# When GpSimd drains at the end of a windowed attention kernel: behind its last instruction, or behind the landing of its own stores

## The chip, the cores and the metric

One core of one Trainium2 chip. The metric is the device time of one execution in microseconds (us), as the median of several runs. Of each kernel one execution was also taken with the hardware profiler; its span (first to last instruction) is about 2 us shorter than its time. Where a kernel was looked at once, its state is called unknown: its time is quoted without a verdict, and the argument rests on its trace alone.

## The reference

Attention within windows of 64 rows, for four sequences of 4096 rows and 1536 columns:

```python
q_w = q.reshape(B, nw, W, D)          # W = 64; k_w and v_w alike
logits = np.einsum('bnwd,bnud->bnwu', q_w, k_w) * D ** -0.5
attn = softmax(logits)                # over the last axis
out = np.einsum('bnwu,bnud->bnwd', attn, v_w).reshape(B, S, D)
```

## The kernel before

The 16,384 rows are worked off in N = 32 blocks of 512. GpSimd issues nearly all transfers: it loads q, k and v of block u + 2 (cast to 16 bits on the way), copies what has landed into the working tiles, and stores the results of block u - 1. Each transfer adds 16 to a semaphore when it has landed. Only the last block is stored by SP (SyncE), in two halves. At the end SP clears all semaphores, and before that GpSimd has to be drained, as a later drain of GpSimd still looks at the semaphores of its transfers. So the drain can be moved, but not just dropped.

```python
for u in range(1, N):
    hand_over("q", u, q16, m_q, g_q)       # wait for the landing, copy, request block u + 2
    hand_over("k", u, k16, m_k, g_k)
    ...                                    # cut: order of the last but two block
    gp.wait_ge(m_q, u + 1)
    store(u - 1)                           # signals d_o[(u - 1) % 3]
    hand_over("v", u, v16, m_v, g_v)
...
for i, c in enumerate((1, 3)):             # the last block, in two halves, by SP
    for a in range(2):
        sy.wait_ge(n_e[a], c)
    sy.dma_start(...).then_inc(d_l[i], 16)
gp.drain()
gp.sem_inc(done, 1)
sy.wait_ge(done, 1)
for i in range(NO):                        # NO = 3
    last = max(u for u in range(N - 1) if u % NO == i)
    sy.wait_ge(d_o[i], 16 * (last // NO + 1))
for i in range(2):
    sy.wait_ge(d_l[i], 16)
sy.sem_clear(range(lo, hi + 1))
```

The softmax here doesn't subtract the row's maximum and nothing guards it: scores larger than these inputs give would overflow.

Of the kernel before, what the change touches and what calls it, by code (L numbers as in the profile page):

```python
# [17 lines left out]
def kernel(  # L18
# [20 lines left out]
    N = B * S // UR  # L39
# [11 lines left out]
    def sem(name):  # L51
        sems.append(nc.alloc_semaphore(name))
        return sems[-1]
# [8 lines left out]
    NO = 3  # L62
# [13 lines left out]
    d_o = [sem(f"d_o{i}") for i in range(NO)]  # L76
# [19 lines left out]
    def rows(x, row0, n, r):  # L96
        return x[row0 : row0 + P * n].rearrange("(h p r) d -> p h (r d)", p=P, r=r)

    def slots(t, lo, hi, r):
        return t[:, lo:hi, :].rearrange("p (h r) d -> p h (r d)", r=r)  # L100

    def load(name, u, dst, s):
        src = {"q": qf, "k": kf, "v": vf}[name]
        r = R if name == "v" else SLOTS
        nc.gpsimd.dma_start(
            out=slots(dst, 0, SLOTS, r), in_=rows(src, u * UR, SLOTS, r)
        ).then_inc(s, 16)
# [176 lines left out]
    def store(u):  # L284
        nc.gpsimd.dma_start(
            out=rows(of, u * UR, SLOTS, SLOTS), in_=slots(outs[u % NO], 0, SLOTS, SLOTS)
        ).then_inc(d_o[u % NO], 16)

    def request(x, u):
        if u < N:  # L290
            load(x, u, landing[x][u % NL], landed[x][u % NL])
# [3 lines left out]
    def hand_over(x, u, dst, m, g):  # L295

        gp = nc.gpsimd
        gp.wait_ge(landed[x][u % NL], 16 * ((u + u % NL) // NL))
        gp.wait_ge(m, u)
        gp.tensor_copy(  # L300
            out=dst[:, :, :].bitcast(FP32), in_=landing[x][u % NL][:, :, :].bitcast(FP32)
        ).then_inc(c_l, 1)
        copies[0] += 1
        gp.wait_ge(c_l, copies[0])
        gp.sem_inc(g, 1)
        request(x, u + NL)

    with tc.tile_critical(no_gpsimd_drain=True):

        nc.sync.dma_start(  # L310
            out=slots(outs[0], 0, SLOTS, SLOTS), in_=rows(qf, 0, SLOTS, SLOTS)
        ).then_inc(d_q0, 16)
        load("k", 0, k16, d_k0)
        nc.vector.memset(ident[:, :], 0.0).then_inc(i_d, 1)
        nc.gpsimd.wait_ge(i_d, 1)
        nc.gpsimd.affine_select(
            out=ident[:, :], in_=ident[:, :], compare_op=mybir.AluOpType.not_equal,
            fill=1.0, base=0, pattern=[[-1, P]], channel_multiplier=1,
        ).then_inc(i_p, 1)
        load("v", 0, v16, d_v0)  # L320
        for u in (1, 2):
            for x in "qkv":
                request(x, u)
        nc.gpsimd.wait_ge(d_q0, 16)
        nc.gpsimd.tensor_copy(out=q16[:, :, :], in_=outs[0][:, :, :]).then_inc(c_q, 1)

        nc.vector.memset(ones[:, :], 1.0).then_inc(i_d, 1)
        nc.vector.memset(zeros[:, :], 0.0).then_inc(i_d, 1)
        for et in ets:
            nc.vector.memset(et[:, :, :, :], 0.0).then_inc(i_d, 1)  # L330
        nc.scalar.wait_ge(i_d, 5)
        nc.scalar.activation(zeros[:, 3:4], zeros[:, 0:1], EXP, bias=zeros[:, 0:1], scale=1.0)

        with nc.Fori(0, N, engines=OrderedEngineSet([PE]), head_slot={PE: 0}):
            tensor_unit()
        assert N % NO == 2
        for eng, unit in ((DVE, vector_unit), (ACT, scalar_unit)):
            with nc.Fori(0, N // NO, engines=OrderedEngineSet([eng]), head_slot={eng: 0}):
                for u in range(NO):
                    unit(u)  # L340
            for u in range(N - 2, N):
                unit(u)

        sy = nc.sync
        for j in range(NJ):
            for n in (2, 3):
                sy.sem_inc(f_o[j][n], 1)
        for a in range(2):
            sy.sem_inc(fr[a], NO)
        sy.sem_inc(f_s[-1], 1)  # L350
        sy.wait_ge(i_p, 1)
        sy.wait_ge(i_d, 5)
        sy.wait_ge(c_q, 1)
        sy.sem_inc(g_q, 1)
        sy.sem_inc(g_k, 1)._wait_ge(d_k0, 16)
        sy.sem_inc(g_v, 1)._wait_ge(d_v0, 16)
        for u in range(NO, N):
            sy.wait_ge(d_o[u % NO], 16 * (u // NO))
            for a in range(2):
                sy.sem_inc(fr[a], 1)  # L360

        gp = nc.gpsimd
        for u in range(1, N):
            hand_over("q", u, q16, m_q, g_q)
            hand_over("k", u, k16, m_k, g_k)
            if u + NL == N - 1:

                hand_over("v", u, v16, m_v, g_v)
            gp.wait_ge(m_q, u + 1)
            store(u - 1)  # L370
            if u + NL != N - 1:
                hand_over("v", u, v16, m_v, g_v)


        last = rows(of, (N - 1) * UR, SLOTS, SLOTS)[:, 0, :]
        for i, c in enumerate((1, 3)):
            for a in range(2):
                sy.wait_ge(n_e[a], c)
            sy.dma_start(
                out=last[:, 2 * i * D : 2 * (i + 1) * D],  # L380
                in_=outs[(N - 1) % NO][:, 2 * i : 2 * (i + 1), :].rearrange("p r d -> p (r d)"),
            ).then_inc(d_l[i], 16)
        gp.drain()
        gp.sem_inc(done, 1)
        sy.wait_ge(done, 1)
        for i in range(NO):
            last = max(u for u in range(N - 1) if u % NO == i)
            sy.wait_ge(d_o[i], 16 * (last // NO + 1))
        for i in range(2):
            sy.wait_ge(d_l[i], 16)  # L390
        lo, hi = min(s.num for s in sems), max(s.num for s in sems)
        assert hi - lo + 1 == len(sems)
        sy.sem_clear(range(lo, hi + 1))
# [30 lines left out]
```

## Time and profile before

| Kernel before | value | where it is read |
|---|---|---|
| time, median | 943.35 us (943.21 to 943.64, 6 runs) | runs |
| DMA engines busy | over 90% in 39 of 40 slices | page, part 2 |
| last landing of a store by GpSimd | 935.37 us | landings in the trace |
| GpSimd's drain | 912.79 to 937.01 us | view of its line |
| last landing of SP's halves | 940.38 us | landings in the trace |
| SP clears the semaphores | 940.47 us | view of its line |

The kernel is a full stream of transfers with a short tail. In the tail three things have to be over before SP may clear: GpSimd's drain, GpSimd's stores, and SP's own two half stores. The latest of them sets the end. How each is found, with the lines, is worked out in the prediction below.

### The profile page before, as it was taken

Reading aid. Unit: us, or ns where it says so; the run is one execution under the profiler, and the core shown is the slowest. Engines: PE = TensorE matmul, PEld = TensorE weight load, DVE = VectorE, ACT = ScalarE, POOL = GpSimd, SP = SyncE. Lnnn points to the kernel's source line nnn. Section 1 sums busy time; section 2 is a strip of 40 time slices with the busy share of each in tenths; the row PEclk is TensorE's granted clock in tenths of the full one; section 3 lists DMA queues with packets and bytes.
Section 4 is the critical chain, followed back from the end, with each engine's and each line's share of the span. In section 5 each row is a group of like instructions: output and inputs, shape, how many; then the busy total and the mean of one; then the engine's idle time right before and its main releaser. Section 6 shows DMA issues by size and latency. Waiting matters only on the chain. (4 is left out here: it accounts for less than half of the span.)

```text
span 941.7 us, 13144 instructions
## 1 busy us (share of the span) xinstructions
PE 644.9 (68%) x5120; PEld 373.5 (40%) x3584; DVE 288.3 (31%) x517; ACT 335.5 (36%) x642; POOL 334.2 (35%) x225
## 2 busy tenths in 40 slices
PE   0877777666766867768666586676776767767683
PEld 0544444433444423445233443334533344334450
DVE  0233333333323332233322233322333223333232
ACT  0344444333333333333333333333333334233331
POOL 4244433344333342333433334333343333443230
PEclk9999999988889788798988999889878889798886
DMA  9999999999999999999999999999999999999997
GB/s 256 219 215 278 265 237 282 283 281 277 231 275 284 280 282 236 266 282 281 283 245 255 283 282 280 256 245 283 282 280 269 233 281 283 282 279 231 273 322 323
DMA packets 22684, 253.35 MB, mean 269 GB/s; under 512 B 2064, under 2 KB 2064, under 8 KB 10256
## 3 DMA queue, kind: packets, MB, share of 16 engines
q0 software_dynamic: 22240, 246.95, 99.7%
q1 hardware_dynamic: 432, 6.29, 1.7%
q14 instruction: 10, 0.08, 0.0%
q8 instruction: 2, 0.03, 0.0%
HBM read 301.99 MB, written 100.66 MB: 428 GB/s over the span
## 5 line engine op out<-in xcount | busy, mean ns | idle before, releaser
L164 PE MATMUL lt<-xq,xk 128*128 128x256 f16 x1536 | 202.6, 281 | 0.0
L300 POOL COPY v<-vl 128x3072 f32<-128x3072 f32 x31 | 85.2, 2749 | 272.4 <-DMA vl<-in_v_dram 272.4
L192 PEld LDWEIGHTS <-et 128*64 128x64 f16 x512 | 40.8, 132 | 331.5 <-issue 317.0
L152 PE MATMUL tp<-ident,q 128*128 128x128 f32 x768 | 109.1, 288 | 80.2 <-DVE xq L228 55.9
L164 PEld LDWEIGHTS lt<-xq,xk 128*128 128x128 f16 x1536 | 152.9, 100 | 26.9
L152 PE MATMUL tp<-ident,k 128*128 128x128 f32 x768 | 125.5, 298 | 54.3 <-PEq L218 37.5
L112 PE MATMUL sp<-ones,et 128*64 128x1 f16 x512 | 52.8, 179 | 146.2 <-PEq L218 126.8
L152 PEld LDWEIGHTS tp<-ident,q 128*128 128x128 f32 x768 | 86.9, 146 | 120.8 <-issue 120.8
L228 ACT COPY xk<-tp 128x512 f32<-128x512 f32 x96 | 59.4, 619 | 199.7 <-ACTq L218 199.7
L152 PEld LDWEIGHTS tp<-ident,k 128*128 128x128 f32 x768 | 96.7, 153 | 71.8 <-issue 69.9
L300 POOL COPY k<-kl 128x3072 f32<-128x3072 f32 x31 | 85.2, 2748 | 102.8 <-DMA kl<-in_k_dram 102.8
L300 POOL COPY q<-ql 128x3072 f32<-128x3072 f32 x31 | 85.0, 2743 | 99.8 <-DMA ql<-in_q_dram 99.8
L245 DVE RECIPROCAL rs<-sp 128x1 f32<-128x1 f32 x128 | 21.3, 166 | 323.9 <-DVEq L218 323.4
L112 PE MATMUL o<-v,et 128*64 128x512 f16 x768 | 118.7, 443 | 0.0
L228 DVE COPY xk<-tp 128x512 f32<-128x512 f32 x96 | 66.4, 692 | 165.4 <-DVEq L218 165.4
L279 ACT ACTIVATE out<-tp,rs 128x512 f32<-128x512 f32 x64 | 44.0, 687 | 177.2 <-ACTq L218 177.2
L269 ACT ACTIVATE et<-lt,zeros 32x128 f16<-32x128 f32 x256 | 91.8, 359 | 39.4 <-ACTq L218 36.1
L228 ACT COPY xq<-tp 128x512 f32<-128x512 f32 x96 | 56.2, 585 | 127.8 <-ACTq L218 127.8
L112 PE MATMUL tp<-v,et 128*64 128x512 f16 x512 | 101.0, 472 | 0.0
L256 DVE TENSOR_SCALAR out<-o,rs 128x512 f32<-128x512 f32 x128 | 90.3, 747 | 28.6 <-DVEq L218 28.1
L228 DVE COPY xq<-tp 128x512 f32<-128x512 f32 x96 | 66.0, 687 | 84.4 <-DVEq L218 84.4
L112 PE MATMUL lt<-v,et 128*64 128x512 f16 x256 | 64.7, 481 | 0.0
(21 smaller groups left out, 217.5 us busy)
## 6 DMA issues: line engine op xcount, KB each, us to landing
out_dram<-out POOLq DMA_DIRECT2D x31, 3072.0 KB, 61.6
ql<-in_q_dram POOLq DMA_DIRECT2D x31, 1536.0 KB, 54.9
kl<-in_k_dram POOLq DMA_DIRECT2D x31, 1536.0 KB, 54.9
vl<-in_v_dram POOLq DMA_DIRECT2D x31, 1536.0 KB, 54.9
out<-in_q_dram SPq DMA_DIRECT2D x1, 3072.0 KB, 16.7
out_dram<-out SPq DMA_DIRECT2D x2, 1536.0 KB, 12.6
k<-in_k_dram POOLq DMA_DIRECT2D x1, 1536.0 KB, 18.0
v<-in_v_dram POOLq DMA_DIRECT2D x1, 1536.0 KB, 24.3
```

The source lines that it names most:

```text
L112: return nc.tensor.add_instruction(mybir.InstMatmult(name=nc.get_next_instruction_name(), engine=PE, ins=[low(rhs), low(w)], outs=[low(o)] ...
L152: ins = nc.tensor.transpose(tps[g % 2][:, r, j, :], pairs[:, c * P : (c + 1) * P], ident[:, :])
L164: ins = nc.tensor.matmul(lts[h][:, r, :, :], lhsT=keys(c, h, r, w), rhs=queries(c, h, w), start=(c == 0 and w == 0 and r == 0), stop=(c == ...
L192: ld = nc.tensor.ldweights(w[h], tile_position=(0, P // H * h))
L228: copy(out=dst, in_=tps[g % 2][:, :, :, :]).then_inc(f_c[g % 4], 1)
L245: ve.reciprocal(out=rs[:, n : n + 1], in_=sp[:, n : n + 1]).then_inc(n_d, 1)
L256: ins = ve.tensor_scalar_mul(scaled(u, n, j), bank(n, j), scalar1=rs[:, n : n + 1])
L269: ins = sc.activation(ets[h][s, :, :, t], lts[h][s, :, :, t], EXP, bias=zeros[s, 0:1], scale=scale)
L279: ins = sc.activation(scaled(u, n, j), bank(n, j), COPY, bias=0.0, scale=rs[:, n : n + 1])
L300: gp.tensor_copy(out=dst[:, :, :].bitcast(FP32), in_=landing[x][u % NL][:, :, :].bitcast(FP32)).then_inc(c_l, 1)
```

## The change

GpSimd's drain comes behind the landing of its own last three stores, in place of right behind its last instruction; the waits for these stores move from SP to GpSimd. The drain no longer sits through some 23 us of transfers in flight.

```diff
+
+        for i in range(NO):
+            last = max(u for u in range(N - 1) if u % NO == i)
+            gp.wait_ge(d_o[i], 16 * (last // NO + 1))
         gp.drain()
         gp.sem_inc(done, 1)
         sy.wait_ge(done, 1)
-        for i in range(NO):
-            last = max(u for u in range(N - 1) if u % NO == i)
-            sy.wait_ge(d_o[i], 16 * (last // NO + 1))
         for i in range(2):
             sy.wait_ge(d_l[i], 16)
```

## The prediction

> **What bounds the kernel now.** I read the page first, for the limit of the whole run, and then only the last 35 us of the trace, since the change touches nothing earlier. The page's second part has the DMA engines busy over 90% in 39 of 40 slices, while PE, the busiest compute engine, is at 68%:
>
> ```profile
> span 941.7 us, 13144 instructions
> PE 644.9 (68%) x5120; PEld 373.5 (40%) x3584; DVE 288.3 (31%) x517; ACT 335.5 (36%) x642; POOL 334.2 (35%) x225
> ...
> DMA  9999999999999999999999999999999999999997
> ```
>
> So the run is a stream of transfers through 16 DMA engines, and its end is set by when the last bytes land. Only the last slice is not full. I therefore cut the tail into stretches (time in us; the two last numbers are DMA share and GB/s):
>
> ```profile
> 928.00:932.00 4.00, 0.00 (x0) 0.00 (x0) 0.00 (x0) 0.00 (x0) 0.00 (x0) 0.50 0.97 414
> 932.00:935.40 3.40, 0.00 (x0) 0.00 (x0) 0.00 (x0) 0.00 (x0) 0.00 (x0) 0.50 0.99 423
> 935.40:936.80 1.40, 0.00 (x0) 0.00 (x0) 0.00 (x0) 0.00 (x0) 0.00 (x0) 0.50 0.40 167
> 936.80:940.40 3.60, 0.00 (x0) 0.00 (x0) 0.00 (x0) 0.00 (x0) 0.00 (x0) 0.50 0.06 27
> 940.40:941.70 1.30, 0.00 (x0) 0.00 (x0) 0.00 (x0) 0.00 (x0) 0.00 (x0) 0.50 0.00 0
> ```
>
> All compute is over by 928. The DMA engines stay full to 935.4; from 936.8 to 940.4 their share is 0.06, which is 1/16: one engine alone is still working off its backlog. Then 1.3 us of clearing semaphores and the closing barrier. The page's own chain of what ended last stops at the last DVE instruction (927.06) and is of no use here; the sync engine's waits show who closes the program:
>
> ```profile
> SPq L390 <- DMA out_dram<-out: 12.9, 2, 9.3
> ```
>
> Line 390 is the wait for the two half stores that SP issues for the last block. It is met at 940.40 in the trace, and only then does SP clear the semaphores. The issue view of the tail (KB each, us from issue to landing) says which stores land there:
>
> ```profile
> out_dram<-out POOLq DMA_DIRECT2D x1, 3072.0 KB, 29.4
> out_dram<-out SPq DMA_DIRECT2D x2, 1536.0 KB, 12.6
> ```
>
> GpSimd's last store is issued at 905.96 and lands at 905.96 + 29.4 = 935.4. SP's two are issued at 924.86 and 927.09; by the view of line 379 they take 11.9 and 13.3 us, so they land at 936.7 and 940.4. The **last landing, 940.4, is SP's store**, 5.0 us after GpSimd's last one.
>
> Finally the drain itself, from the view of its source line (duration min/median/max in ns, first and last start), and as a comparison three closing drains on the same engine after everything has landed:
>
> ```profile
> L383 POOLq DRAIN  x1: 24227/24227/24227, 912.8 to 912.8; - x1
> ```
> ```profile
> L419 POOLq DRAIN  x3: 34/40/78, 940.7 to 941.4; - x3
> ```
>
> The drain starts at 912.785, right behind the last copy (909.92 + 2.75 = 912.67), and ends at 912.785 + 24.227 = 937.01. That is 1.6 us after GpSimd's last store landed and 3.4 us before SP's.
>
> **What the Trainium skill says.** "Perfetto Trace Analysis", section "Sequencer-only Instruction (DRAIN, etc)": the profile's window of such an instruction covers its execution and leaves out the semaphore wait. The trace agrees: the drain's record starts when the copy's semaphore wait is over, so the 24.2 us are the drain executing. "PSUM — Partial Sum Buffer", section "Engine vs sequencer instructions": "drain waits for the engine to go fully idle". GpSimd's last counted instruction ended at 912.67, so by busy time alone the drain should be short; the trace has 24.2 us, and the page doesn't say that stores in flight are waited for. "DMA: Bandwidth & Descriptors", section "Issuing engines are not separate DMA queues": transfers from SP and GpSimd interleave on the same 16 engines. The trace agrees, with a share of 0.97 to 0.99 while both queues have work (928 to 935.4). The same page, "Latency and other measured facts", calls two DMA engines usually slower and guesses, as uncertain, at contention for the port where GpSimd's descriptor rings lie. The trace has one late engine: of the 16 landings of the last store, fifteen are in by 937.92 and the last at 940.38.
>
> **The change part by part.** *Removed*: up to three waits on SP (17 to 28 ns each in the trace). All three stores concerned have landed by 935.4, before SP's last wait is met at 940.4, so they cost the end nothing now. *Added*: the same three waits on GpSimd ahead of its drain. The first two are met at 917.5 and 925.1, the last at 935.4, each handled in about 0.02 us. *Moved*: the start of the drain, from 912.8 to about 935.5. Instructions per engine stay the same otherwise; the instruction order shows no other difference than line numbers.
>
> New time of the signal from GpSimd to SP = 935.4 (landing) + 0.1 (waits) + d, where d is what a drain costs when nothing of its own is in flight. It is on the path only if it comes later than 940.4, that is if d exceeds 4.9 us. Three readings of d: 0.04 us, if it is like the closing drains; about 1.6 us, if the stretch between landing and the drain's end is a cost that follows a landing; 24.2 us, if the drain's time had nothing to do with the stores. With the first two the signal comes at 935.5 or 937.1, against 937.0 now, with 4.9 or 3.3 us to spare. SP then still waits to 940.4, and the sum is 0.0 us. The profiled execution was 943.48 us in time for a span of 941.7; both should repeat: 943.4.
>
> **The rivals.** *One: the drain is busy waiting, and that slows the DMA engines.* If GpSimd's cores look again and again at the descriptor rings while it drains, 24 us of that disappear, and the late engine could be less late. For it: between fifteenth and last landing the distance is 1.09 us at the last load before the drain (909.9), then 1.42, 1.79 and 2.46 us for stores that land during it. Against it: a store after loads already adds about 0.2 us to this distance long before any drain (1.02 to 1.24 us near 881), and three stores in a row without loads between them occur nowhere else. If all growth since 909.9 were the drain's, the gain would be 2.46 - 1.09 = 1.4 us, giving 942.0; if only the excess over 0.2 us per 3 MB, 1.37 - 4 x 0.2 = 0.6 us (four such amounts: three stores of 3 MB and the two halves together), giving 942.8. I give a visible gain one chance in five; neither size nears 2%.
>
> *Two: the drain has a fixed cost, or one that grows with the number of transfers issued, and it ran hidden behind the stores.* Then 24.2 us start at 935.5, the signal comes at 959.7, 19.3 us after 940.4, and the time is 962.7: 2.0% slower, right at the boundary. Against it: the end of the drain follows the landing by 1.6 us, which would be chance, and the closing drains take 0.03 to 0.08 us. For it: those come after a drain that may already have done the accounting, and no other drain in this trace meets transfers. I give it 3%. A milder form, with d between 5 and 15 us, would give 943.5 to 953.5; another 3%.
>
> *Three: the new wait takes the old one's place and nothing moves.* That is my main case: it differs from rival one only in saying that the drain disturbs nothing.
>
> **Range and chances.** Main case 943.4, a fifth of a chance at some 0.6 to 1.4 us less, a few per cent at much more. The runs of before spread over 0.4 us, and I allow about 1 us for another build or moment. Predicted 943.3, range 942.1 to 944.8. Faster by over 2% needs 18.9 us out of a tail in which DMA engines are idle for only about 5: 0.005. Slower by over 2% is rival two in full: 0.02. Within 2%: 0.975.
>
> **What would show it right or wrong.** In the profile after, the drain should start near 935.5 and last under 2 us: that shows it was waiting for stores, and refutes rival two. SP's wait for its own half stores should again be the last, near 940.4, with the clearing of semaphores 0.1 us behind it. The stretch in which one DMA engine works alone should keep its 3.6 us; if it shrinks by half a microsecond or more, and the distance of the last landing from the fifteenth with it, rival one is right. The prediction fails if the drain takes over 5 us behind the landing, or if SP's last wait is met by GpSimd's signal in place of its own store.

## The result, and the profile after

The changed kernel takes 943.57 us (943.23 to 943.67, 6 runs) against 943.35 us (943.21 to 943.64, 6 runs) before: ratio 1.0001, interval [0.9989, 1.0014]. Nothing moved. The page of the profile after:

```profile
span 941.6 us, 13143 instructions
PE 640.9 (68%) x5120; PEld 370.3 (39%) x3584; DVE 288.4 (31%) x517; ACT 336.0 (36%) x642; POOL 334.6 (36%) x225
...
DMA  9999999999999999999999999999999999999997
```

The busy times are those of before within 1%, and the DMA row is the same digit for digit. The tail in the same stretches (us, then the engines' busy times, granted clock, DMA share, GB/s):

```profile
932.00:935.40 3.40, 0.00 (x0) 0.00 (x0) 0.00 (x0) 0.00 (x0) 0.00 (x0) 0.50 0.99 423
935.40:936.80 1.40, 0.00 (x0) 0.00 (x0) 0.00 (x0) 0.00 (x0) 0.00 (x0) 0.50 0.42 176
936.80:940.40 3.60, 0.00 (x0) 0.00 (x0) 0.00 (x0) 0.00 (x0) 0.00 (x0) 0.50 0.09 38
```

Full to 935.4, nearly idle from 936.8: the same tail. The last stores, by who issues them (KB each, median us from issue to landing):

```profile
out_dram<-out POOLq DMA_DIRECT2D x1, 3072.0 KB, 30.3
out_dram<-out SPq DMA_DIRECT2D x2, 1536.0 KB, 14.4
```

GpSimd's is issued at 905.87 us and lands at 936.14. SP's halves take 13.7 and 15.2 us; the second, issued at 925.10, lands at 940.26. Who lets SP go is in SP's waits after 920 us (line waiting, whom it waited for, us in total, times, longest):

```profile
SPq L391 <- DMA out_dram<-out: 14.8, 1, 14.8
...
SPq L394 <- POOLq L387: 0.2, 1, 0.2
```

Line 391 is again the wait for SP's own halves, met at 940.27 us. Line 394 is the clearing, which now also has to wait for the signal behind the drain (line 387). Its 0.2 us are no loss: the record of the clearing starts at 940.35 us, less than 0.1 us after that of line 391, just as before. The drain itself and the closing drains behind it (ns min/median/max, then first and last start in us):

```profile
L387 POOLq DRAIN  x1: 3249/3249/3249, 936.2 to 936.2; - x1
```
```profile
L420 POOLq DRAIN  x3: 34/40/78, 940.6 to 941.3; - x3
```

Here is the surprise behind an unchanged time. GpSimd's last store lands at 936.14 us, the drain starts at 936.16, **and although nothing of GpSimd's is in flight any more it takes 3.25 us**. Its signal comes at 939.41, only 0.85 us ahead of SP's last landing at 940.26. Before, the drain was over at 937.01 us, 3.4 us ahead. The change has spent three quarters of a reserve without showing it in the time. So the experiments ask what the 3.25 us are, and when they would come into sight.

### The profile page after: what moved, and what is told of

Same layout as the page of the kernel before. It is cut to its first block, busy times and chain, and to the rows that moved or that the text cites. A ratio compares the mean times of both kernels' runs of the same rounds, so it can differ in the third digit from the quotient of the medians.

```text
span 941.6 us, 13143 instructions
## 1 busy us (share of the span) xinstructions
PE 640.9 (68%) x5120; PEld 370.3 (39%) x3584; DVE 288.4 (31%) x517; ACT 336.0 (36%) x642; POOL 334.6 (36%) x225
## 5 line engine op out<-in xcount | busy, mean ns | idle before, releaser
L152 PE MATMUL tp<-ident,k 128*128 128x128 f32 x768 | 122.8, 294 | 55.7 <-PEq L218 38.1
L152 PEld LDWEIGHTS tp<-ident,k 128*128 128x128 f32 x768 | 94.7, 151 | 72.7 <-issue 70.7
```

The source lines that it names most:

```text
L152: ins = nc.tensor.transpose(tps[g % 2][:, r, j, :], pairs[:, c * P : (c + 1) * P], ident[:, :])
```

## The experiments

Twelve kernels ran, all with correct results. Unless told otherwise each is an edit of the changed kernel.

### Put the drain behind everything: is it a cost, or other traffic?

```diff
+        for i in range(2):
+            gp.wait_ge(d_l[i], 16)
         gp.drain()
```

> GpSimd waits for SP's two half stores as well, so the drain starts at about 940.3 us with no transfer left in flight anywhere. Theory A (bookkeeping over all transfers that GpSimd issued since its last drain, done after the landing where the drain starts late): the drain again takes about 3.2 us, all of it on the path, and the time is 943.5 + 3.3 = 946.8 us, 1.0035 of before. Theory B (the 3.2 us came from transfers of SP running at that moment): the drain takes under 0.5 us, and the time is 943.5 to 944.0 us. Theory C (a fixed cost of any drain that follows transfers): as A.

Measured: 947.05 us against 943.85 us of the kernel before on the same chip, ratio 1.0034 [1.0020, 1.0048]. The view of the drain's line, then SP's waits in the tail:

```profile
L389 POOLq DRAIN  x1: 3249/3249/3249, 941.0 to 941.0; - x1
```
```profile
SPq L393 <- DMA out_dram<-out: 13.5, 1, 13.5
...
SPq L396 <- POOLq L389: 3.5, 1, 3.5
```

With every transfer landed the drain takes the same 3249 ns to the nanosecond, and now SP's clearing waits 3.5 us for it. Theory B (SP's traffic) falls. The cost is the drain's own, and fully exposed it is worth 3.2 us, 0.34% of this kernel.

### Two drains in a row: is it paid per drain?

```diff
         gp.drain()
+        gp.drain()
```

> Two drains in a row behind GpSimd's own stores. First one as in the changed kernel, 936.2 to 939.4 us. Theory A: the second has nothing to account for and takes under 0.1 us; time unchanged at 943.5 us. Theory B: the second lasts until the traffic is over or is short, at most 0.9 us. Theory C: the second takes 3.2 us as well, the signal comes at about 942.7 in place of 940.3, and the time is about 945.9 us.

Measured (one look): 943.29 us. The first drain, then the second:

```profile
L387 POOLq DRAIN  x1: 3249/3249/3249, 936.1 to 936.1; - x1
```
```profile
L388 POOLq DRAIN  x1: 40/40/40, 939.3 to 939.3; - x1
```

The second takes 0.04 us. Theory C (a fixed cost of each drain) falls; the first drain settles something that is then settled.

### A drain ahead of the last store

```diff
-            store(u - 1)
+            if u < N - 1:
+                store(u - 1)
 ...
+        gp.drain()
+        store(N - 2)
```

> A drain ahead of GpSimd's last store, which is issued late for that, and the final drain behind its landing: the final drain has one transfer to account for in place of 126. The first drain starts at about 912.7 and ends some 1.6 us after the second last store lands at 925.1, so about 926.7; the last store then lands near 941 us. Theory A: the final drain takes under 0.3 us. Theory C: it takes 3.2 us. Theory B: it depends on what is still in flight, likely under 0.5 us since SP's stores will be done. The time is about 1.5 us longer for the hole in the transfers, plus the final drain.

Measured (one look): 944.45 us. The final drain has one transfer to settle:

```profile
L391 POOLq DRAIN  x1: 129/129/129, 941.3 to 941.3; - x1
```

So the cost hangs on transfers issued since the drain before. The early drain of this kernel ends at 926.90 us, 1.60 us behind the landing (925.30) that it had waited for. SP's two stores were in flight then (issued at 924.50 and 926.72 us, landed at 930.01 and 937.62): GpSimd's drain waited for GpSimd's own transfers, not for SP's.

### Start the drain while one store is still in flight

```diff
-        for i in range(NO):
+        for i in (1, 2):
```

> GpSimd waits for all its stores but the last, so the drain starts at about 925.1 us, with one of its own stores still in flight until about 935.4 to 936.1. Theory A: the bookkeeping of what has landed is done while the last store flies, and the drain ends 1.6 us behind the landing as in the kernel before (near 937.3). Theory C with a fixed cost behind the landing: it ends 3.2 us behind it. Theory B: no rule, the end depends on SP's transfers. The time stays at 943.5 us in each.

Measured (one look): 943.71 us.

```profile
L387 POOLq DRAIN  x1: 11775/11775/11775, 925.5 to 925.5; - x1
```

The drain starts at 925.45 and lasts 11.775 us, to 937.23; the last store lands at 935.58, 1.64 us earlier. In the kernel before the drain ends 1.64 us behind the landing. So a drain that starts early pays part of its 3.25 us while it waits, whether it starts 23 us or 10 us ahead, and a remainder of half stays behind the landing. Both kernels stay at their time, since that end is still before SP's last landing (940.59).

### More transfers for the same bytes

Each of GpSimd's 95 loads is issued as two halves, once on the changed kernel and once on the kernel before:

```diff
-        nc.gpsimd.dma_start(
-            out=slots(dst, 0, SLOTS, r), in_=rows(src, u * UR, SLOTS, r)
-        ).then_inc(s, 16)
+        o, i = slots(dst, 0, SLOTS, r), rows(src, u * UR, SLOTS, r)
+        for a in range(2):
+            ...                       # oa, ia: half a of both
+            nc.gpsimd.dma_start(out=oa, in_=ia).then_inc(s, 16)
```

(The waits for these semaphores count to 32 for a load in place of 16.)

> The changed kernel with each of GpSimd's 95 loads issued as two halves of 768 KB: 31 + 190 = 221 transfers in place of 126, the same bytes. Theory A by transfers: from 0.129 us for one and 3.249 us for 126, one more costs 0.025 us; the drain takes 0.129 + 220 x 0.025 = 5.6 us. Theory A by packets (bytes): the drain stays at 3.2 us as long as the packets do. If 5.6: it starts at about 936.1 and its signal comes at 941.7, 1.4 us after SP's stores, so it sets the end: time 1.4 us above its sister with the drain in the old place.

> The kernel before with the same split of the loads. Theory A by transfers: the drain starts near 912.7 and ends 1.65 x 221 / 126 = 2.9 us behind the landing of GpSimd's last store, at about 939.0, still hidden behind SP's stores at 940.3; time as before, 943.5 us, if the split itself costs the transfers nothing. By packets: 1.65 us behind the landing.

Measured: 946.82 us for the changed kernel with split loads, 946.96 us for its sister, against 943.59 us of the kernel before: 1.0034 and 1.0035. **The expectation missed twice.** The split costs 3.3 us for both (the last store of GpSimd lands at 938.83 and 938.85 us in place of some 936; why was not pursued), and the drain got cheaper, not dearer:

```profile
L391 POOLq DRAIN  x1: 2102/2102/2102, 938.9 to 938.9; - x1
```

With 221 transfers in place of 126 the drain takes 2.1 us. A cost for every transfer issued since the start is refuted, and so is one for every packet: the page counts 31,824 in GpSimd's queue, in place of 22,240. The sister's drain ends at 939.92 us, 1.07 us behind the landing: half of 2.1 once more.

### An extra drain halfway

```diff
         for u in range(1, N):
+            if u == N // 2:
+                gp.drain()
             hand_over("q", u, q16, m_q, g_q)
```

> One more drain halfway, ahead of the hand-over of block 16, when GpSimd has issued 68 transfers; 58 come after it. It costs tens of us, as it stops GpSimd until all in flight has landed, and that isn't the question. Theory A by transfers since the last drain: the final drain takes 0.129 + 57 x 0.025 = 1.55 us. If it is a fixed cost for more than one transfer, or counts from the start of the program, it takes 3.2 us. The midway drain should end 1.65 x 68 / 126 = 0.9 us behind the landing that it waited for.

Measured (one look): 955.46 us, since GpSimd stands still halfway for 57.7 us. The final drain:

```profile
L389 POOLq DRAIN  x1: 4794/4794/4794, 946.9 to 946.9; - x1
```

58 transfers since the last drain cost more than 126 did: 4.8 us. The expected 1.55 us missed by a factor of three, and so did the 0.9 us for the midway drain: it ends 2.83 us behind the landing that it had waited for. But (4.794 - 0.040) / 58 = 0.082 us, close to the (0.129 - 0.040) = 0.089 us of the single transfer. That suggested a different theory, A2: the drain pays 0.082 us for each transfer whose bookkeeping is still *open*, and while the program runs, older ones are closed now and then in bulk. (Bookkeeping, open and closed are names for what the times suggest; no trace shows that work itself.) The 3.249 us would then stand for (3.249 - 0.040) / 0.082 = 39 open transfers, the 2.102 us for 25.

### No drain and no clearing

```diff
-        gp.drain()
-        sy.sem_clear(range(lo, hi + 1))
```

> GpSimd's own drain is left out, and so is SP's clearing of the semaphores, which may not come ahead of it; the program's closing drain on GpSimd, which took 0.04 us so far, is the first one behind the transfers. Theory A: the closing drain inherits the bookkeeping, takes 3.2 us at about 940.7, and the time is 946.5 us. If a closing drain does no bookkeeping: 0.04 us and 943.4 us.

Measured: 946.37 us against 943.59 us of the kernel before, ratio 1.0028 [1.0013, 1.0044]. All drains of the program's closing line:

```profile
L418 POOLq DRAIN  x3: 46/78/3249, 940.9 to 944.6; - x3
```

The closing drain, 0.04 us elsewhere, inherits the 3249 ns and puts them on the path. Leaving out one's own drain saves nothing; it moves the bill to the worst place.

### Testing the second theory by numbers

Four kernels, each with the number of open transfers set by an extra drain ahead of block 24 (with split loads), 10 (in the order of after and of before) and 6. The edit is that of the drain halfway with another block number.

> Theory A as it stood (0.025 us for every transfer since the last drain) has fallen: 221 transfers took 2.1 us, 58 took 4.8. Theory A2 in its place: the drain pays about 0.082 us for each transfer whose bookkeeping is still open, (4.794 - 0.040) / 58, and while the program runs older ones are closed in bulk whenever some store of fixed size is full; by this the 3.249 us stand for 39 open transfers and the 2.102 us for 25. Here the loads are split and a drain stands ahead of block 24, so exactly 44 transfers come after it, with 396 descriptors per DMA engine (8 for the data of each and 1 for its signal, from the packets on the page). A2 by transfers: the final drain takes 0.04 + 44 x 0.082 = 3.65 us. A2 by descriptors (4.754 us for 634 in the run with the drain at block 16, 0.0075 us each): 3.0 us.

> The changed kernel with a drain ahead of block 10: 82 transfers come after it, 898 descriptors per engine. A2, if the store that forces a bulk closing holds about 1024 descriptors per engine (an estimate: 93 of 126 transfers before a closing, at 11 each): none is closed before the end, and the final drain takes 0.04 + 82 x 0.082 = 6.8 us. It then ends after SP's stores, which land 4.2 to 5.5 us behind GpSimd's, and sets the end: the time is 1.5 to 2.5 us over its sister with the drain in the old place. If closings come at random or by time: anything between 1 and 4 us.

> The kernel before with the same extra drain ahead of block 10. A2 with half of the work done while the last store flies (the drain halfway ended 2.83 us behind its landing with 68 open transfers, half of 68 x 0.082): the final drain ends 3.4 us behind the landing, still hidden behind SP's stores. Its time is 1.5 to 2.5 us under its sister's.

> The changed kernel with a drain ahead of block 6: 98 transfers come after it, 1074 descriptors per engine, just over the estimated 1024. A2: one bulk closing a few transfers from the end leaves those still in flight then (about 8) and the 4 or 5 after it open, so the final drain takes 0.04 + 12 x 0.082 = 1.0 us (0.7 to 1.6). Without such a limit: 0.04 + 98 x 0.082 = 8.1 us.

Measured, the final drain's line of the kernels with block 24 (split; one look, 957.76 us), block 10 in the order of after, and block 6 (one look, 953.81 us):

```profile
L393 POOLq DRAIN  x1: 3647/3647/3647, 948.5 to 948.5; - x1
```
```profile
L389 POOLq DRAIN  x1: 6754/6754/6754, 946.1 to 946.1; - x1
```
```profile
L389 POOLq DRAIN  x1: 1282/1282/1282, 945.7 to 945.7; - x1
```

Expected were 3.65, 6.8 and 1.0 (0.7 to 1.6) us. The first decides that the bill goes by transfers and not by descriptors (which would have given 3.0 us). The second and third stand on both sides of the estimated limit: 82 transfers cost 6.8 us and 98 cost 1.3, as they should if a bulk closing near the end leaves few open. The closing itself is inferred from this fall.

The pair with block 10 shows what the order is worth when the drain is dear: 956.47 us (955.89 to 957.21, 4 runs) in the order of after, 954.25 us (954.20 to 954.34, 4 runs) in the order of before, on the same chip. By the means, 956.51 / 954.26 = 1.0024, and the runs don't overlap. SP's waits in the tail, first of the order of after and then of the order of before:

```profile
SPq L393 <- DMA out_dram<-out: 12.9, 1, 12.9
...
SPq L396 <- POOLq L389: 1.9, 1, 1.9
```
```profile
SPq L392 <- DMA out_dram<-out: 13.3, 2, 9.7
```

The drain in the order of before:

```profile
L385 POOLq DRAIN  x1: 25710/25710/25710, 923.9 to 923.9; - x1
```

In the order of after, SP's halves land at 951.06 us and the clearing waits 1.9 us more for the drain, which ends at 952.83. In the order of before the drain ends at 949.62, 3.40 us behind its landing (946.22) and 1.6 us ahead of SP's halves (951.24); no wait for it is listed. **Here the changed order is slower by 2.2 us**, of which these two traces show 1.7 in the clearing: its record starts 1.79 us behind SP's last landing, against 0.08 in the order of before.

All drains that started with everything of GpSimd's landed, in one table:

| kernel | transfers since the last drain | drain, us | open, by 0.04 + 0.082 each |
|---|---|---|---|
| second of two drains | 0 | 0.040 | 0 |
| drain ahead of the last store | 1 | 0.129 | 1 |
| split loads, block 24 | 44 | 3.647 | 44 |
| halfway (block 16) | 58 | 4.794 | 58 |
| block 10 | 82 | 6.754 | 82 |
| block 6 | 98 | 1.282 | 15 |
| changed kernel | 126 | 3.249 | 39 |
| split loads | 221 | 2.102 | 25 |

From 44 to 82 the slope is (6.754 - 3.647) / 38 = 0.082 us. And the drains that started with a store still in flight, each as the time from that landing to the drain's end, beside half of what the open ones cost: kernel before 1.64 (1.6), drain after two stores 1.64 (1.6), split loads in the old order 1.07 (1.05), halfway 2.83 (68 open: 2.8), block 10 in the old order 3.40 (3.4). The other extra drains agree, though no expectation was recorded for them: ahead of block 10 they end 1.85 us behind the landing (44 open: 1.8) in both orders, ahead of block 6 1.2 us (28 open: 1.2).

What is shown: the cost per transfer up to 82, its fall beyond, and the half. The open ones of the last three rows are worked out from the drains themselves, so they test nothing. What stays open: whether it is a bulk closing that makes the cost fall, and when it happens. An estimate from the packets on the page (8 per engine and one for the signal for each store and load of q and k, 16 and one for v: 1390 in all) says about 1000 descriptors per engine, which fits the last three rows but was not measured by itself. The extra drain ahead of block 24 with split loads leans the same way: it ends 3.27 us behind its landing, which by the half stands for 79 open of 177, so 98 of these smaller transfers would have been closed, against 83 and 87 of the whole ones in the rows of block 6 and the changed kernel. Why half is left behind the landing is open as well.

## Why the prediction was right or wrong

- *The end is set by SP's last half store, 5.0 us behind GpSimd's, and the DMA stream fixes both*: right, and this is why nothing moved. After, the two landings are at 936.14 and 940.26 us, 4.1 us apart, and SP clears 0.1 us behind the second.
- *The drain waits for stores in flight, so it is short once they have landed*: the first half is right, 24.2 us became 3.2. The second is where a term was mis-sized. The prediction had three readings of d, "0.04 us", "about 1.6 us" and "24.2 us", and a limit of 4.9 us. Measured: 3.249 us, none of the three. The signal came at 939.41 rather than at 935.5 or 937.1.
- *Which step misled*: taking the 1.6 us between landing and end of the drain as the whole cost that follows a landing. It is what is left of it for a drain that began early; one that begins late pays twice that. The closing drains were a bad comparison for the reason that the prediction itself named against them: the drain ahead of them had done the accounting.
- *The stated check "last under 2 us"* failed, and yet the time held, as 3.249 is below 4.9 and below the 4.1 us actually there. The prediction's time was right with 0.85 us to spare, less than it claimed (3.3 or 4.9). That d lay under the limit was in part luck: none of its readings lay between 1.6 and 24.2 us, and it gave a d from 5 to 15 us, beyond the limit, only 3%.
- *Rival two, "a fixed cost, or one that grows with the number of transfers issued"*: its full size is refuted (24.2 us did not reappear), its mechanism is partly right: the cost grows with transfers, 0.082 us each, but not with all that were issued (by theory A2 only with those still open), and was at most 6.75 us in these runs. The prediction gave a milder form 3%, with d of at least 5 us; at d = 6.75 (block 10) the order does cost 2.2 us.
- *Rival one, the drain disturbs the late DMA engine*: refuted, though half of its stated sign appeared: the distance of the last landing from the fifteenth shrank from 2.46 to 1.59 us. But the two executions differed by as much ahead of any drain: at the last load the distance was 1.09 us before and 0.26 after. The growth since then is nearly the same: 1.38 us before, with a drain under way, 1.33 us after, without one, and 1.33 and 1.32 us in the two kernels without a drain before SP's last landing (the drain behind everything; no drain and no clearing). Others vary more, but not with the drain: growth was 0.88 us with one under way (block 10, old order), and the distance shrank by 0.97 us with none (halfway). From that load's last landing to the last of all it took 30.52 us before and 30.49 after. So the drain is not what makes the last landing late.
- *Two readings of the tail that were off*, without harm to the time: the prediction's 3.6 us with "one engine alone" are a window with several engines at its start, as the last landing is alone only for 2.46 us; and its row of distances leaves out GpSimd's last store (3.38 us) and ends with SP's halves (2.46), the second of which landed after the drain was over.
- *Moving three waits costs nothing*: right; after, two of them are one instruction of 0.04 us at 925.1, the drain itself carries the third, and none is on the path.

## What to carry to other kernels

In these runs a drain of GpSimd was a wait for its transfers plus a bill: 0.082 us for each of up to 82 transfers since the last drain, and less in all for more of them. Begun early, while the last stores were still in flight, it had half of that bill paid out of sight. A wait that looks long because it starts early is often free, and starting it late can turn hidden work into a serial step: before moving it, look at what is done during the wait and how far the next engine's signal is behind. No version here beats the two kernels: their end is set by SP's last landing, which no place of the drain brought forward.

## What the Trainium skill lacked or had wrong

- "PSUM — Partial Sum Buffer", section "Engine vs sequencer instructions", says that a drain waits for the engine to go fully idle. On GpSimd it also waits for the transfers that GpSimd issued: it lasted 24.2 us behind the last counted instruction, to 1.6 us behind the last landing. In another kernel it was over while SP's stores were still in flight. The page doesn't say so.
- No page has the bill of such a drain: 0.040 us with nothing open, 0.129 us for one transfer, 6.754 us for 82, and the same 3249 ns for the 126 of this kernel in four runs. "DMA: Bandwidth & Descriptors" describes how GpSimd's descriptors are made, not what closing them costs.
- "VectorE: DVE Perf Modes", section "The DRAIN you can't avoid", takes the drains of the program's closing part for boilerplate of about 12 ns, constant on all engines. Here GpSimd's took 34 to 78 ns, and one took 3249 ns where it was the first behind the transfers.
- "DMA: Bandwidth & Descriptors", section "Latency and other measured facts", calls two engines usually slower and guesses why, but doesn't say by how much. Here one landing of the last store comes 2.46 us behind the fifteenth before the change and 1.59 us after it. The runs don't name the engine and don't test the guess.
